# Moving four modulation chunks from TensorE to VectorE and sharing weight pieces between two streams at the ends of stages

## The chip, the cores and the metric

The kernel runs on one NeuronCore of a Trainium2 chip, as one program in one launch. The metric is the device time of that launch in microseconds (us). Of the core's engines TensorE (PE) multiplies matrices and transposes, VectorE (DVE) does elementwise work and row statistics, ScalarE (ACT) applies functions and scaled copies, GpSimd (POOL) does little here but issue some DMAs, and the sync engine (SP) issues the DMAs that bring weights from HBM.

## The reference

A first block (a hybrid attention layer, not touched here) makes x of 256 tokens x 1024 channels. Then a second block of two layers works on two streams, the latent x and a context of 256 tokens:

```python
for l in range(2):
    mod_l = silu(c) @ ada_w[l] + ada_b[l]        # 9 chunks of 1024: shift, scale, gate x 3; c is one vector
    mod_c = silu(c_ctx) @ ada_w[l] + ada_b[l]    # the same for the context
    xl = layer_norm(ALPHA*xl + 0.5*g1 * swiglu(xl*(1+sc1)+sh1, ffn1_w_in[l], ffn1_w_out[l]))
    xc = the same with the context's chunks
    yc, yl = even_mixer(...) if l == 0 else odd_mixer(...)     # linear attention + MLA, or neighbourhood attention
    xl = layer_norm(ALPHA*xl + g2 * yl)
    xl = layer_norm(ALPHA*xl + 0.5*g3 * swiglu(xl*(1+sc3)+sh3, ffn2_w_in[l], ffn2_w_out[l]))
    # in layer 0 xc takes the last two steps too; in layer 1 only xl does
```

All of it is in float32, with a hidden width of 2816 in the feed-forwards.

## The kernel before

**Streams and products.** X and C are the two streams, two tiles of 128 tokens each. In the code who=1 is C and who=0 is X; `order` is C first, then X. Every product is made of split numbers: a factor is a high part plus a low part, and `mm3` (L434 to L436) issues three matmuls for one product, high x high, low x high and high x low. A weight piece is 128 x 1024 floats, 512 KB. `wload` brings it: SP issues the DMA into `wr` (`wraw`), ACT casts it to `wh` (L353), DVE subtracts to get `wl` (L428), and then PE uses both. There are four buffers each of `wr`, `wh` and `wl`.

**Stages.** ff1 (name "f1", l=0), then the even mixer (`even_first`, scans, attention, and `mixer_out`), then ff2 (name "f2", l=0), then f1 of layer 1, the odd mixer (its value projection is `odd_values`), and f2 of layer 1 for X alone. `ffn_two` walks over 22 hidden tiles in groups of 8, 8 and 6. A call of `ffn_in` makes one hidden tile from two weight pieces; for both streams together (512 tokens) that is 48 matmuls of 128x512. In the first three hidden tiles of a stage (F0) the streams go one after the other at 256 tokens, and each loads the pieces for itself. `ffn_out` multiplies a group with the output weights, in two halves n=0 and n=1 of 512 channels.

**The end of a stage.** After the last group the kernel does C's n=0, C's n=1, then X's n=0, X's n=1, each with pieces of its own. `accum` (L571ff: L575 multiplies by the gate row, L579 or L577 adds to the stream), `layernorm` (L580ff: statistics L587, reciprocal root L367 to L377, normalisation L592) and `xt_mod` (L545ff: transposes L527 on PE, modulation L558, high part on ACT, low part XTL by L560) follow for each stream. For some streams (table `TL`) n=1 goes through `tail`, which takes the second tile in smaller column parts. `mixer_out` has the same shape with 8 pieces for each stream, `odd_values` with 8 for each stream too.

**Modulation.** A chunk (l, c) is 1024 columns of ada_w[l]. `ada` computes it on PE: 64 float32 matmuls with two useful rows (L620), and for a chunk that is no gate two transposes (L635). `ada_v` computes it on DVE: for each of 8 pieces two operations (L660, one for c and one for c_ctx) that multiply a 128x1024 piece by a broadcast row and sum along it; 16 in a chunk. Lists V1, V2 and V3 say which chunks DVE takes, in ff1, in ff2 of layer 0 and in f1 of layer 1. `fillv` takes VR[..][0] pieces after every `ffn_in` of the stage from the sixth on and VR[..][1] after steps of `ffn_out`; what is left of a list is emitted at the head of the stage's end (`self.fillv(1000)`). Chunks of neither list are taken by `fill`, on PE, in ff1 and in the even mixer.

**What sets the order.** The program is written in the order above, with `defer` moving `xt_mod` a few weight loads later. A scheduler of the tile framework then orders each engine's instructions by priority and estimated readiness; on the chip each engine works through its list in that order.

Of the kernel before, what the change touches and what calls it, by code (L numbers as in the profile page):

```python
# [20 lines left out]
P = 128  # L21
D = 1024
KD = 8
NFT = 22
# [178 lines left out]
GX = 0.0  # L203
DF = (3, 3, 3, 4, 2)
TL = (1, 0, 0, 0, 1, 1, 0, 0, 1)
# [13 lines left out]
ROWS = 1  # L219
# [24 lines left out]
class Kern:  # L244
# [95 lines left out]
    def need(self, l, c):  # L340

        while (l, c) not in self.done:
            if (l, c) in V1 + V2 + V3:
                self.fillv(1)
# [370 lines left out]
        for _ in self.ffn_in_steps(*a):  # L715
            pass

    def ffn_in_steps(self, wi, ft, hid, ts, hs, pool, tag, share=None):

        nc = self.nc  # L720
        N = ts.stop - ts.start
        if N == 256:
            b = self.bank(tag)
            pgu = (b[:, :256], b[:, 256:])
        else:
            pgu = (self.bank(tag), self.bank(tag))
        for j in range(2):
            h, lo = self.wload(wi, (2 * ft + j) * 1024, 1024, share)
# [8 lines left out]
        self.split(hid[:, 0, hs], hid[:, 1, hs], pgu[1])  # L737
        yield

    def ffn_out(self, wo, n, f0, f1, hid, tiles, tag, early={}):  # L740
# [25 lines left out]
        for (z, gb, c0), o in zip(tiles, outs):  # L766
            self.accum(z, n, o, gb, f0 == 0)

    def tail(self, rows, mul, gb, first, tag, done=None):


        nc = self.nc
        for m, z in enumerate(rows):
            st = self.small([P, 3, 6], "lnst3", bufs=2)
            nc.vector.bn_stats(st[:, 0], z[:, :512])
            parts = ((0, 256), (256, 512)) if m else ((0, 512),)
            for i, (a, b) in enumerate(parts):
                o = self.bank(tag)
                mul(o[:, a:b], m, a, b)
                t = o[:, a:b]  # L780
# [12 lines left out]
            nb = self.small([P, 1], "lnnb")  # L793
            nc.vector.scalar_tensor_tensor(nb, mv[:, 0:1], -1.0, y, op0=OP.mult, op1=OP.mult)
            h = slice(0, D)
            if m:
                h = slice(512, D)
                nc.vector.tensor_scalar(z[:, :512], z[:, :512], mv[:, 0:1], y, op0=OP.subtract, op1=OP.mult)
            self.act(z[:, h], z[:, h], AF.Identity, scale=y, bias=nb)
            if done:  # L800
                done(m)

    def ffn_tail(self, wo, f0, hid, tiles, done=None):

# [61 lines left out]
    def ffn_two(self, name, l, pool, order, after, fills=(0, 0), vr=(0, 0), early={}):  # L866


        self.pnext = PNF[2 * l + int(name[1]) - 1]
        gbs = {}  # L870
        wi, wo = self.A[name + "i"][l], self.A[name + "o"][l]
        G, F0 = 8, F2[l]
        if early:
            F0 = len(early) + FE
        for f0 in range(0, NFT, G):
            f1 = min(f0 + G, NFT)
            hid = []
# [3 lines left out]
            if f0 == 0:  # L881
                for w in order:
# [3 lines left out]
                    for ft in range(0 if w == 0 else len(early), F0):  # L886
                        self.ffn_in(wi, ft, hid[ft], ts, ts, pool, "B", GX)
# [30 lines left out]
    def mixer_out(self, src, l, who, pool):  # L918
        self.pnext = PN[4]
        gb = self.gate_rows(l, 1, who, pool)  # L920
        rows = (self.X, self.C)[who]
        outs = self.xs(src, 0, 512, 256 * who, 2)
        for m in range(2):
            self.accum(rows[m], 0, outs[m], gb, True)
        if TL[6 + who]:
            self.xs_tail(src, 4096, 256 * who, rows, gb)
        else:
            outs = self.xs(src, 4096, 512, 256 * who, 2, rows=ROWS)
            for m in range(2):
                self.accum(rows[m], 1, outs[m], gb, True)  # L930
            self.layernorm(rows)


    def rope(self, v, cos, sin, half, tag):
# [825 lines left out]

    def odd_values(self, e, order):
        V = [self.tl(e, [P, D], f"nv{m}") for m in range(4)]
        for w in order:
            for n in range(2):
                outs = self.xs(self.A["na"], 16 * 1024 + n * 4096, 512, 256 * w, 2)
                for m in range(2):
                    self.copy_any(V[2 * w + m][:, n * 512:(n + 1) * 512], outs[m])
        return V

    def odd(self, e, V):  # L1770
# [47 lines left out]
    def run(self):  # L1818
        tc, nc, A = self.tc, self.nc, self.A
        stage = self.stage or 99  # L1820
# [45 lines left out]
        with tc.tile_pool(name="xd", bufs=1) as xc:  # L1866
# [1 line left out]
            for i, t in enumerate(self.X + self.C):  # L1868
                nc.gpsimd.dma_start(t, save[i])
            with tc.tile_pool(name="mo", bufs=1) as g:  # L1870
                self.gbn, self.accp = 1, g
                self.mixer_out(A["evo"], 0, 1, g)
                if stage > 5:
                    self.defer(lambda: self.xt_mod(0, 6, 1), DF[2])
                self.mixer_out(A["evo"], 0, 0, g)
                if stage > 5:
                    self.defer(lambda: self.xt_mod(0, 6, 0), DF[3])
            if stage == 5:
                return self.store()
            self.gbn, self.phase = 2, 1  # L1880
# [10 lines left out]
            with tc.tile_pool(name="nm", bufs=1) as e:  # L1891
# [3 lines left out]
                with tc.tile_pool(name="na", bufs=1) as e2:  # L1895
                    V = self.odd_values(e2, (1, 0))
# [5 lines left out]
                gb = self.gate_rows(1, 1, 0, e)  # L1902
                outs = self.xs(A["nao"], 0, 512, 0, 2, xh=self.NH, xl=self.NL, tag="P")
# [4 lines left out]
                else:  # L1908
                    outs = self.xs(A["nao"], 4096, 512, 0, 2, xh=self.NH, xl=self.NL, tag="P", rows=ROWS)
# [78 lines left out]
```

## Time and profile before

| | us |
|---|---|
| median of 3 runs | 2183.82 (2181.91 to 2188.89) |
| the profiled execution, by its own clock | 2177.1 |
| its span from first to last instruction | 2175.3 |
| PE busy | 2097.1 (96%) |
| DVE busy | 1512.4 (70%) |
| ACT busy | 868.0 (40%) |

The profile is of one execution. Busy time is the time in which an engine's instructions run; PE is busy for nearly all of the span, so what PE is given to do, and the few places where it stands idle, make up the time. In the rows below, a number in square brackets behind an instruction is the time that its engine stood idle before it, with the event that ended the wait. [...]

### The profile page before, as it was taken

What the parts mean: (1) busy time and instruction counts of PE and PEld (TensorE: products, weight loads), DVE (VectorE), ACT (ScalarE), POOL (GpSimd) and SP (SyncE); (2) the same over time, 40 slices, a digit from 0 to 9 for tenths busy, and PEclk for the clock granted to TensorE, in tenths of its full rate; (3) what the DMA queues carried; (4) which work ended last, traced back from release to release, by engine and by line L of the source; (5) the groups of instructions that cost most, each with busy time, mean ns of one, the idle gap of its engine ahead of it and who ended that gap; (6) DMA issues with size and microseconds to landing.
All of it is one profiled execution on the core that took longest, in us unless ns stands there. A gap on an engine that the chain in (4) does not pass through costs nothing.

```text
span 2175.3 us, 31944 instructions
## 1 busy us (share of the span) xinstructions
PE 2097.1 (96%) x12484; PEld 1769.3 (81%) x12484; DVE 1512.4 (70%) x2746; ACT 868.0 (40%) x1493; POOL 40.0 (2%) x78
## 2 busy tenths in 40 slices
PE   7999999999999899998999999899999989998998
PEld 5898798888877787887888888888888868887997
DVE  6977866667778775868466656846665676776666
ACT  5555545222223534544322223532222255654443
POOL 1000000000000000000000000000000010000000
PEclk9999999999999999999999999999999999998999
DMA  8545547656665312347444545544453364424663
GB/s 283 194 149 177 158 145 245 205 176 202 201 203 178 100 57 67 119 147 240 134 126 146 164 118 154 174 126 136 140 170 113 110 188 145 105 86 138 188 182 123
DMA packets 94903, 337.84 MB, mean 155 GB/s; under 512 B 11357, under 2 KB 12477, under 8 KB 94753
## 3 DMA queue, kind: packets, MB, share of 16 engines
q1 hardware_dynamic: 87552, 314.78, 46.8%
q0 software_dynamic: 5856, 17.39, 2.7%
q10 hardware_dynamic: 1344, 3.64, 0.5%
q8 instruction: 98, 1.61, 0.3%
q14 instruction: 53, 0.43, 0.1%
HBM read 332.94 MB, written 3.20 MB: 155 GB/s over the span
## 4 chain that ended last, share of the span: by engine, by line
PE 87%; DVE 7%; DMA 2%; ACT 2%; issue 2%; SPq 0%; ACTq 0%; DVEq 0%
PE pB L434 13%; PE pB L436 12%; PE pB L435 12%; PE pA L436 10%; PE pA L435 10%; PE pA L434 10%; PE pB L1483 2%; PE pF L434 2%; PE pF L436 2%; PE pF L435 2%; DVE wl L428 1%; PE pP L434 1%; PE pP L435 1%; PE pP L436 1%; DMA wr<-in_ada_dram 1%
## 5 line engine op out<-in xcount | busy, mean ns | idle before, releaser
L353 ACT ACTIVATE wh<-wr 128x1024 fp32r<-128x1024 f32 (+4 forms) x460 | 480.2, 1047 | 1022.5 <-issue 490.8
L428 DVE TENSOR_TENSOR wl<-wr,wh 128x1024 fp32r<-128x1024 f32 (+4 forms) x460 | 553.1, 1204 | 335.6 <-ACT wh L353 332.2
L434 PE MATMUL pB<-XTH,wh 128*128 128x512 f32 (+1 forms) x1552 | 539.3, 348 | 6.8 <-DVE hid L441 4.0
L436 PE MATMUL pB<-XTH,wl 128*128 128x512 f32 (+1 forms) x1552 | 535.3, 345 | 5.6 <-DVE wl L428 5.6
L435 PE MATMUL pB<-XTL,wh 128*128 128x512 f32 (+1 forms) x1552 | 535.6, 345 | 0.4 <-DVE XTL L560 0.4
L434 PEld LDWEIGHTS pB<-XTH,wh 128*128 128x128 f32 x1552 | 294.5, 190 | 48.5 <-DVE hid L441 4.4
L436 PEld LDWEIGHTS pB<-XTH,wl 128*128 128x128 f32 x1552 | 294.5, 190 | 43.9 <-DVE wl L428 5.8
L435 PEld LDWEIGHTS pB<-XTL,wh 128*128 128x128 f32 x1552 | 294.4, 190 | 38.2 <-DVE XTL L560 0.6
L435 PE MATMUL pA<-wl,hid 128*128 128x512 f32 (+1 forms) x624 | 239.5, 384 | 2.6 <-DVE wl L428 2.6
L436 PE MATMUL pA<-wh,hid 128*128 128x512 f32 (+1 forms) x624 | 239.5, 384 | 0.0
L434 PE MATMUL pA<-wh,hid 128*128 128x512 f32 (+1 forms) x624 | 238.0, 383 | 0.0
L660 DVE SCALAR_TENSOR_TENSOR vj<-wr,cb 128x1024 f32<-128x1024 f32 x176 | 214.9, 1221 | 11.7 <-DMA wr<-in_adav_dram 8.3
L736 DVE TENSOR_TENSOR pB<-ft,pB 128x512 f32<-128x512 f32 (+1 forms) x97 | 55.7, 574 | 136.2 <-PE pB L436 134.9
L435 PEld LDWEIGHTS pA<-wl,hid 128*128 128x128 f32 x624 | 117.2, 188 | 27.3 <-DVE wl L428 3.8
L434 PEld LDWEIGHTS pA<-wh,hid 128*128 128x128 f32 x624 | 117.1, 188 | 24.9 <-issue 0.6
L436 PEld LDWEIGHTS pA<-wh,hid 128*128 128x128 f32 x624 | 117.2, 188 | 22.8
L435 PE MATMUL pA<-wl,XTH 128*128 128x512 f32 (+4 forms) x336 | 125.0, 373 | 5.6 <-DVE wl L428 5.5
L434 PE MATMUL pA<-wh,XTH 128*128 128x512 f32 (+4 forms) x336 | 125.6, 376 | 0.4 <-ACT wh L353 0.4
L436 PE MATMUL pA<-wh,XTL 128*128 128x512 f32 (+4 forms) x336 | 125.5, 374 | 0.0
L575 DVE TENSOR_TENSOR pA<-pA,gb 128x512 f32<-128x512 f32 x84 | 58.0, 695 | 31.9 <-PE pA L436 31.7
L435 PEld LDWEIGHTS pA<-wl,XTH 128*128 128x128 f32 x336 | 64.7, 193 | 17.3 <-DVE wl L428 6.9
L434 PEld LDWEIGHTS pA<-wh,XTH 128*128 128x128 f32 x336 | 64.9, 193 | 12.3 <-ACT wh L353 0.7
(456 smaller groups left out, 2949.3 us busy)
## 6 DMA issues: line engine op xcount, KB each, us to landing
wr<-in_f1i_dram SPq DMA_DIRECT2D x108, 512.0 KB, 4.4
wr<-in_f2i_dram SPq DMA_DIRECT2D x94, 512.0 KB, 4.0
wr<-in_adav_dram SPq DMA_DIRECT2D x88, 512.0 KB, 3.9
wr<-in_ada_dram SPq DMA_DIRECT2D x56, 512.0 KB, 4.3
wr<-in_f1o_dram SPq DMA_DIRECT2D x56, 512.0 KB, 3.7
wr<-in_f2o_dram SPq DMA_DIRECT2D x50, 512.0 KB, 3.6
wr<-in_w_dram SPq DMA_DIRECT2D x40, 512.0 KB, 4.3
wr<-in_na_dram SPq DMA_DIRECT2D x32, 512.0 KB, 3.6
```

The costliest lines, as they stand in the source:

```text
L353: self.lasta = self.nc.scalar.activation(out, in_, func, **kw)
L428: i = eng.tensor_sub(lo[:, :w], raw[:, :w], h[:, :w].bitcast(F32))
L434: nc.tensor.matmul(out, lh, rh, start=start, stop=False)
L435: nc.tensor.matmul(out, lh, rl, start=False, stop=False)
L436: self.lastmm = nc.tensor.matmul(out, ll, rh, start=False, stop=stop)
L575: nc.vector.tensor_mul(p, p, gb[:, cs])
L660: nc.vector.scalar_tensor_tensor(junk, raw, 0.5 * f, cb[:, w], op0=OP.mult, op1=OP.mult, accum_out=gc[:, w, k:k + 1])
L736: nc.vector.tensor_mul(pgu[1], t, pgu[1])
L1483: nc.tensor.matmul(p[:, c0 + j * P:c0 + (j + 1) * P], K[r, j * 256 + tk * P:j * 256 + (tk + 1) * P], Q[r, j * 256 + tq * P:j * 256 + (tq + ...
```

## The change

**Modulation.** Chunks (0,6), (0,7), (0,8) and (1,1), which PE computed, go to DVE: V1 has 6 chunks in place of 5, V2 has 4 in place of 3, V3 has 5 in place of 3. PE keeps only chunks (0,0) to (0,2), which are done during the first block. The rates rise from 2.0, 1.25 and 1.25 pieces to 2.4, 1.75 and 2.2.

**Weight pieces.** At the end of a stage the new `both_out` loads the pieces of n=0 once for C and X (`row_products`), and then the pieces of n=1 once, for C and then for X. So C's second half comes after X's first half. C's `xt_mod` is emitted at X's first product of n=1. `mixer_out` uses the same function and loads both gate rows ahead (`gbn` 2). In the first three hidden tiles of a stage the last tile's two pieces are kept from C for X (`keep`). `odd_values` makes C n=0, C n=1, X n=1 with C's pieces, and X n=0. In all 36 of 432 pieces of 128x1024 fall away.

```diff
-V1 = ((0, 3), (0, 4), (0, 5), (1, 0), (1, 2))
-V2 = ((1, 3), (1, 4), (1, 5))
-V3 = ((1, 6), (1, 7), (1, 8))
-VR = ((2.0, 0.5), (1.25, 0.25), (1.25, 0.25))
+V1 = ((0, 3), (0, 4), (0, 5), (0, 6), (0, 7), (0, 8))
+V2 = ((1, 0), (1, 1), (1, 2), (1, 3))
+V3 = ((1, 4), (1, 5), (1, 6), (1, 7), (1, 8))
+VR = ((2.4, 0.5), (1.75, 0.25), (2.2, 0.25))
...
+    def row_products(self, ws, mul, tiles, n, first, tag, hook=None):
+        for i, (z, gb, _) in enumerate(tiles):
+            o = self.bank(tag)
+            mul(o, i, 0, 512)
+            if hook and i == 0:
+                hook()
+            self.accum(z, n, o, gb, first)
+
+    def both_out(self, pieces, mul, streams, first, ends, tag, after):
+        ws = pieces(0)
+        alls = streams[0][1] + streams[1][1]
+        self.row_products(ws, lambda o, i, a, b: mul(ws, o, alls[i], a, b), alls, 0, first, tag)
+        w1 = pieces(1)
+        for i, (rows, tiles) in enumerate(streams):
+            def hook():
+                if i == 1:
+                    with self.tc.issue_after(self.lastmm.ins):
+                        after(0)
+            def m1(o, m, a, b):
+                mul(w1, o, tiles[m], a, b)
+            if ends[i]:
+                self.tail(rows, m1, tiles[0][1], first, tag, hook=hook)
+            else:
+                self.row_products(w1, m1, tiles, 1, first, tag, hook)
+                self.layernorm(rows)
+        after(1)
...
                 self.fillv(1000)
-                for w in order:
-                    for _ in self.ffn_out(wo, 0, f0, f1, hid, tiles(w), "A"):
-                        pass
-                    if TL[2 * (2 * l + int(name[1]) - 1) + w]:
-                        self.ffn_tail(wo, f0, hid, tiles(w))
-                    else:
-                        for _ in self.ffn_out(wo, 1, f0, f1, hid, tiles(w), "A"):
-                            pass
-                        self.layernorm((self.X, self.C)[w])
-                    self.defer(lambda w=w: after(w), DF[0] if w else DF[1])
+                us = range(f0, NFT, 2)
...
+                k = 2 * (2 * l + int(name[1]) - 1)
+                self.both_out(lambda n: [self.wload(wo, (n * NFT + u) * 512, 1024) for u in us], mul,
+                              [((self.X, self.C)[w], tiles(w)) for w in order], False, [TL[k + w] for w in order], "A",
+                              lambda i: self.defer(lambda: after(order[1]), DF[1]) if i else after(order[0]))
```

The instruction lists show the new order at three places. First DVE at the end of ff1, before. `vj` rows are operations of the modulation (here a gate chunk), `wl` rows the low parts of weight pieces, `lnst` the statistics of C's rows:

```order
L660 SCALAR_TENSOR_TENSOR vj_4862,vg_6570<-wr_6757,cb_4859 128x1024
L579 TENSOR_TENSOR C_4_98<-C_4_98,pA_6768 128x512
L660 SCALAR_TENSOR_TENSOR vj_4862,vg_6570<-wr_6757,cb_4859 128x1024
L428 TENSOR_TENSOR wl_6845<-wr_6841,wh_6843 128x1024
L666 SCALAR_TENSOR_TENSOR vg_6570<-adabc,vg_6570 128x16
L587 BN_STATS lnst_6888<-C_3_97 128x6
L587 BN_STATS lnst_6905<-C_4_98 128x6
L428 TENSOR_TENSOR wl_6927<-wr_6923,wh_6925 128x1024
```

The same place in the changed kernel, where the `pA` rows are the gate multiplications of C's second half:

```order
L660 SCALAR_TENSOR_TENSOR vj_4850,vg_6452<-wr_6545,cb_4847 128x1024
L428 TENSOR_TENSOR wl_6671<-wr_6667,wh_6669 128x1024
L660 SCALAR_TENSOR_TENSOR vj_4850,vg_6452<-wr_6545,cb_4847 128x1024
L428 TENSOR_TENSOR wl_6677<-wr_6673,wh_6675 128x1024
L660 SCALAR_TENSOR_TENSOR vj_4850,vg_6452<-wr_6549,cb_4847 128x1024
L587 BN_STATS lnst_6739<-C_4_98 128x6
L660 SCALAR_TENSOR_TENSOR vj_4850,vg_6452<-wr_6549,cb_4847 128x1024
L575 TENSOR_TENSOR pA_6679<-pA_6679,gb_4859 128x512
L666 SCALAR_TENSOR_TENSOR vg_6452<-adabc,vg_6452 128x16
L575 TENSOR_TENSOR pA_6700<-pA_6700,gb_4859 128x512
```

Eight operations of the modulation stood behind the last hidden tile of the stage (its L441) before, thirteen stand there now, and the kept pieces of n=1 (`wl_6671`, `wl_6677`) stand among the last of them. Second PE at the same place, before. `pF` with `ident` are transposes of C, `pA_7045` and `pA_7085` are X's second half:

```order
L434 MATMUL pA_7045<-wh_7033,hid_6243 128x512
L435 MATMUL pA_7045<-wl_7035,hid_6243 128x512
L527 MATMUL pF_6981<-ident,C_3_97 128x128
L527 MATMUL pF_6992<-ident,C_3_97 128x128
L436 MATMUL pA_7045<-wh_7033,hid_6243 128x512
L434 MATMUL pA_7045<-wh_7033,hid_6244 128x512
L435 MATMUL pA_7045<-wl_7035,hid_6244 128x512
L436 MATMUL pA_7045<-wh_7033,hid_6244 128x512
L434 MATMUL pA_7045<-wh_7039,hid_6245 128x512
L435 MATMUL pA_7085<-wl_7029,hid_6241 128x256
L436 MATMUL pA_7085<-wh_7027,hid_6241 128x256
```

And in the changed kernel, where `pA_6863` is the last part of X's second half and `pA_6909` and `pA_6940` belong to `even_first`:

```order
L435 MATMUL pA_6863<-wl_6677,hid_6065 128x256
L436 MATMUL pA_6863<-wh_6675,hid_6065 128x256
L527 MATMUL pF_6776<-ident,C_3_97 128x128
L527 MATMUL pF_6787<-ident,C_3_97 128x128
L527 MATMUL pF_6776<-ident,C_4_98 128x128
L527 MATMUL pF_6776<-ident,C_3_97 128x128
L527 MATMUL pF_6776<-ident,C_4_98 128x128
L527 MATMUL pF_6787<-ident,C_4_98 128x128
L527 MATMUL pF_6787<-ident,C_3_97 128x128
L527 MATMUL pF_6787<-ident,C_4_98 128x128
L434 MATMUL pA_6909<-XTH,wh_6905 32x256
L434 MATMUL pA_6940<-XTH,wh_6936 128x256
```

Before, C's transposes stood within X's products; now all of X's products stand ahead of them. Third DVE at the end of f1 of layer 1, before, where `pA_15367` is X's last column part and `wl_15425` the first piece of `odd_values`:

```order
L786 TENSOR_TENSOR X_1120_9407<-X_1120_9407,pA_15367 128x256
L560 TENSOR_TENSOR XTL<-pF_15274,XTH 128x256
L375 TENSOR_SCALAR nwt_15332<-nwy_15331,lnv_15329 128x1
L787 BN_STATS lnst_15343<-X_1120_9407 128x6
L376 TENSOR_SCALAR nwt_15332<-nwt_15332 128x1
L428 TENSOR_TENSOR wl_15425<-wr_15421,wh_15423 128x1024
L377 TENSOR_SCALAR nwy_15331<-nwt_15332,nwy_15331 128x1
L789 BN_AGGR lnmv_15389<-lnst_15343 128x2
L428 TENSOR_TENSOR wl_15443<-wr_15439,wh_15441 128x1024
```

And in the changed kernel, where `wl_14999` is the first piece of `odd_values` and `X_1064` X's second tile with its first half:

```order
L575 TENSOR_TENSOR pA_14670<-pA_14670,gb_12965 128x512
L579 TENSOR_TENSOR X_1063_9019<-X_1063_9019,pA_14670 128x512
L428 TENSOR_TENSOR wl_14722<-wr_14718,wh_14720 128x1024
L428 TENSOR_TENSOR wl_14728<-wr_14724,wh_14726 128x1024
L575 TENSOR_TENSOR pA_14691<-pA_14691,gb_12965 128x512
L428 TENSOR_TENSOR wl_14999<-wr_14995,wh_14997 128x1024
L579 TENSOR_TENSOR X_1064_9020<-X_1064_9020,pA_14691 128x512
L793 TENSOR_TENSOR pA_14732<-pA_14732,gb_12963 128x512
```

The first piece of `odd_values` stood behind X's last addition before; now it stands ahead of the end of X's first half, before anything of X's second half.

## Rows read from the trace of the kernel before

**Rows 1.** Page, part 1: busy us (share of the span) xinstructions.

```profile
PE 2097.1 (96%) x12484; PEld 1769.3 (81%) x12484; DVE 1512.4 (70%) x2746; ACT 868.0 (40%) x1493; POOL 40.0 (2%) x78
```

**Rows 2.** Four stretches of stages: length, busy us by engine, PEclk, DMA share, GB/s.

```profile
364.00:640.00 276.00, 276.00 (x1551) 228.38 (x1550) 193.37 (x278) 74.35 (x98) 0.50 (x1) 1.00 0.62 194
...
843.00:906.00 63.00, 60.78 (x495) 47.97 (x494) 48.56 (x91) 30.18 (x57) 1.14 (x2) 0.92 0.39 128
...
1026.00:1343.00 317.00, 316.57 (x1431) 259.98 (x1430) 191.41 (x260) 85.12 (x110) 0.50 (x1) 1.00 0.47 139
...
1404.00:1723.00 319.00, 319.00 (x1450) 261.35 (x1449) 192.09 (x260) 84.02 (x106) 0.50 (x1) 1.00 0.46 135
```

**Rows 3.** Line L620 alone in two stretches: PE and weight-load busy us (records).

```profile
340.00:668.00 328.00, 11.10 (x320) 8.26 (x320) 1.00 0.64 207
...
843.00:906.00 63.00, 8.76 (x192) 5.40 (x192) 0.92 0.39 128
```

**Rows 4.** PE in order of time around one burst of L620: start, duration, instruction.

```profile
642.21 0.39 PE L435 MATMUL pB<-XTL,wh 128*128 128x512 f32 x1
...
643.15 0.40 PE L436 MATMUL pB<-XTH,wl 128*128 128x512 f32 x1
643.47 1.08 PE L620 MATMUL pF<-wr,cs 128*32 128x128 f32 x32
...
644.82 0.39 PE L435 MATMUL pB<-XTL,wh 128*128 128x512 f32 x1
```

**Rows 5.** PE at the end of ff1, with its idle time in brackets.

```profile
684.13 0.49 PE L435 MATMUL pA<-wl,hid 128*128 128x512 f32 x1 [1.18 <-DVE wl L428]
...
711.72 0.55 PE L434 MATMUL pA<-XTH,wh 128*128 128x256 f32 x1 [3.56 <-DVE nwt L373]
```

**Rows 6.** DVE just ahead of that first wait.

```profile
681.71 1.22 DVE L660 SCALAR_TENSOR_TENSOR vj<-wr,cb 128x1024 f32<-128x1024 f32 x1
...
682.85 1.22 DVE L428 TENSOR_TENSOR wl<-wr,wh 128x1024 fp32r<-128x1024 f32 x1
```

**Rows 7.** DVE by line from 668 to 713.4 us: busy us, mean ns of one.

```profile
L428 DVE TENSOR_TENSOR wl<-wr,wh 128x1024 fp32r<-128x1024 f32 (+1 forms) x10 | 11.3, 1126 | 0.2 <-ACT wh L353 0.2
L660 DVE SCALAR_TENSOR_TENSOR vj<-wr,cb 128x1024 f32<-128x1024 f32 x8 | 9.8, 1219 | 0.0
L575 DVE TENSOR_TENSOR pA<-pA,gb 128x512 f32<-128x512 f32 x6 | 4.1, 692 | 0.0
L560 DVE TENSOR_TENSOR XTL<-pF,XTH 128x256 fp32r<-128x256 f32 x8 | 3.2, 417 | 0.1
...
L587 DVE BATCH_NORM_STATS2 lnst<-C 128x6 f32<-128x512 f32 x4 | 2.6, 680 | 0.0
...
L592 DVE TENSOR_SCALAR C<-C,lnmv,nwy 128x1024 f32<-128x1024 f32 x2 | 1.6, 804 | 0.0
...
L375 DVE TENSOR_SCALAR nwt<-nwy,lnv 128x1 f32<-128x1 f32 x3 | 0.8, 267 | 0.0
```

**Rows 8.** PE at the end of the even mixer, with its idle time.

```profile
1018.20 0.77 PE L527 MATMUL pF<-ident,X 128*128 128x128 f32 x5 [2.65 <-DVE X L592]
```

**Rows 9.** PE at the end of ff2 of layer 0, with its idle time.

```profile
1383.97 0.58 PE L436 MATMUL pB<-XTH,wl 128*128 128x256 f32 x1 [5.56 <-DVE wl L428]
```

**Rows 10.** PE at the end of f1 of layer 1 and in odd_values, with its idle time.

```profile
1763.74 0.80 PE L435 MATMUL pA<-wl,XTH 128*128 128x512 f32 x1 [5.00 <-DVE wl L428]
...
1782.12 0.88 PE L527 MATMUL pF<-ident,X 128*128 128x128 f32 x3 [3.98 <-DVE XTL L560]
```

**Rows 11.** ACT in that stretch: the cast of a piece of odd_values.

```profile
1773.08 1.06 ACT L353 ACTIVATE wh<-wr 128x1024 fp32r<-128x1024 f32 x1 [6.70 <-DMA wr<-in_na_dram]
```

**Rows 12.** Three stretches of 20 us around those ends, columns as in rows 2.

```profile
700.00:720.00 20.00, 14.90 (x99) 12.80 (x98) 18.27 (x50) 9.46 (x17) 1.75 (x5) 0.83 0.44 134
...
1380.00:1400.00 20.00, 16.02 (x116) 16.03 (x117) 18.29 (x43) 8.02 (x15) 0.00 (x0) 0.83 0.61 189
1760.00:1780.00 20.00, 14.41 (x56) 11.37 (x56) 12.98 (x33) 7.12 (x10) 5.26 (x9) 0.83 0.94 265
```

More of the change, by code (lines that the diff above doesn't have):

```diff
@@ L716, in ffn_in, with ffn_in_steps @@
             pass
-    def ffn_in_steps(self, wi, ft, hid, ts, hs, pool, tag, share=None):
+    def ffn_in_steps(self, wi, ft, hid, ts, hs, pool, tag, share=None, ws=None):
         nc = self.nc
         N = ts.stop - ts.start
+        new = []
         if N == 256:
@@ L727, in ffn_in_steps @@
         for j in range(2):
-            h, lo = self.wload(wi, (2 * ft + j) * 1024, 1024, share)
+            if ws and len(ws) == 2:
+                h, lo = ws[j]
+            else:
+                h, lo = self.wload(wi, (2 * ft + j) * 1024, 1024, share)
+                if ws is not None:
+                    new.append((h, lo))
             self.ws(pgu[j], h, lo, ts)
@@ L737, in ffn_in_steps @@
         self.split(hid[:, 0, hs], hid[:, 1, hs], pgu[1])
+        if new:
+            ws += new
         yield
@@ L767, in ffn_out, with tail @@
             self.accum(z, n, o, gb, f0 == 0)
-    def tail(self, rows, mul, gb, first, tag, done=None):
+    def tail(self, rows, mul, gb, first, tag, done=None, hook=None):
         nc = self.nc
@@ L779, in tail @@
                 mul(o[:, a:b], m, a, b)
+                if hook and m == 0:
+                    hook()
                 t = o[:, a:b]
@@ L881, in ffn_two @@
             if f0 == 0:
+                keep = []
                 for w in order:
@@ L885, in ffn_two @@
                         self.flush()
-                    for ft in range(0 if w == 0 else len(early), F0):
-                        self.ffn_in(wi, ft, hid[ft], ts, ts, pool, "B", GX)
+                    fs = list(range(0 if w == 0 else len(early), F0))
+                    if keep:
+                        fs = fs[-1:] + fs[:-1]
+                    for ft in fs:
+                        self.ffn_in(wi, ft, hid[ft], ts, ts, pool, "B", GX, keep if ft == F0 - 1 else None)
             for ft in range(f0 if f0 else F0, f1):
@@ L918, in mixer_out @@
-    def mixer_out(self, src, l, who, pool):
-        self.pnext = PN[4]
[L920 to L931, printed above, removed]
+                us = range(f0, NFT, 2)
@@ new lines, in mul @@
+                def mul(ws, o, t, a, b):
+                    for u, w in zip(us, ws):
+                        for j in range(2):
+                            hh, s = hid[u + j - f0], slice(t[2], t[2] + P)
+                            js = slice(j * 512 + a, j * 512 + b)
+                            self.mm3(o, hh[:, 0, s], hh[:, 1, s], w[0][:, js], w[1][:, js], u + j == f0, u + j == NFT - 1)
+                k = 2 * (2 * l + int(name[1]) - 1)
+                self.both_out(lambda n: [self.wload(wo, (n * NFT + u) * 512, 1024) for u in us], mul,
+                              [((self.X, self.C)[w], tiles(w)) for w in order], False, [TL[k + w] for w in order], "A",
+                              lambda i: self.defer(lambda: after(order[1]), DF[1]) if i else after(order[0]))
@@ new lines, in mixer_out, with mul @@
+    def mixer_out(self, src, l, pool, after):
+        self.pnext = PN[4]
+        streams = []
+        for w in (1, 0):
+            gb = self.gate_rows(l, 1, w, pool)
+            rows = (self.X, self.C)[w]
+            streams.append((rows, [(rows[m], gb, 256 * w + m * P) for m in range(2)]))
+        def mul(ws, o, t, a, b):
+            s = slice(t[2], t[2] + P)
+            for k in range(8):
+                w, js = ws[k // 2], slice(k % 2 * 512 + a, k % 2 * 512 + b)
+                self.mm3(o, self.XTH[:, k, s], self.XTL[:, k, s], w[0][:, js], w[1][:, js], k == 0, k == 7)
+        self.both_out(lambda n: [self.wload(src, n * 4096 + 1024 * u, 1024) for u in range(4)], mul, streams, True,
+                      (TL[7], TL[6]), "A", after)
@@ L1762, in odd_values, with put @@
         V = [self.tl(e, [P, D], f"nv{m}") for m in range(4)]
-        for w in order:
-            for n in range(2):
-                outs = self.xs(self.A["na"], 16 * 1024 + n * 4096, 512, 256 * w, 2)
-                for m in range(2):
-                    self.copy_any(V[2 * w + m][:, n * 512:(n + 1) * 512], outs[m])
+        src, o = self.A["na"], 16 * 1024
+        a, b = order
+        def put(w, n, outs):
+            for m in range(2):
+                self.copy_any(V[2 * w + m][:, n * 512:(n + 1) * 512], outs[m])
+        put(a, 0, self.xs(src, o, 512, 256 * a, 2))
+        ws = []
+        for w in (a, b):
+            outs = [self.pA(), self.pA()]
+            for u in range(4):
+                if w == a:
+                    ws.append(self.wload(src, o + 4096 + u * 1024, 1024))
+                elif u == 0:
+                    self.flush()
+                for m in range(2):
+                    s = slice(256 * w + m * P, 256 * w + (m + 1) * P)
+                    for j in range(2):
+                        js = slice(j * 512, (j + 1) * 512)
+                        self.mm3(outs[m], self.XTH[:, 2 * u + j, s], self.XTL[:, 2 * u + j, s], ws[u][0][:, js], ws[u][1][:, js],
+                                 u + j == 0, u == 3 and j == 1)
+            put(w, 1, outs)
+        put(b, 0, self.xs(src, o, 512, 256 * b, 2))
         return V
@@ L1870, in run @@
             with tc.tile_pool(name="mo", bufs=1) as g:
[L1871 to L1877, printed above, removed]
+                self.gbn, self.accp = 2, g
+                self.mixer_out(A["evo"], 0, g, lambda i: self.defer(lambda: self.xt_mod(0, 6, 0), DF[3]) if i
+                               else self.xt_mod(0, 6, 1))
             if stage == 5:
```

2 lines of the change are left out of this document (added).

## The prediction, as put on record

> **What bounds the kernel now.** I began with the page's busy times: PE is busy for 96% of the span, DVE for 70% [rows 1]. So time is won by giving PE less to do or by filling its gaps, and DVE has room on the average only. The next view was busy time by stretch. In the middle of the three feed-forwards that carry modulation on DVE, PE is busy for all of the time and DVE for 193.37 of 276, 191.41 of 317 and 192.09 of 319 us [rows 2]. Then PE in order of time with its idle gaps. These lie at the ends of stages, where one stream's last products, its layer norm, its transposes and the next stage's first product follow each other: 1.18 and 3.56 us at the end of ff1 [rows 5], 2.65 at the end of the even mixer [rows 8], 5.56 at the end of ff2 [rows 9], 5.00 and 3.98 around odd_values [rows 10]. All these end with something of DVE. Last, the clock there: it is granted at 0.83 on average over 20 us at three of the ends [rows 12], so PE fell to the lower of its levels for part of them, and (1 - 0.83) x 20 = 3.4 us of work is lost beside the gap, at most.
>
> **Modulation off PE.** A burst of L620 has 32 records. From the matmul before it (643.15) to the second one after it (644.82) pass 1.67 us [rows 4]; two 128x512 matmuls alone take 2 x 0.235 = 0.47, since four steps from 642.21 to 643.15 take 0.94 [rows 4]. So a burst costs 1.20 us, and a hidden tile of 48 matmuls takes 11.3 us. In ff1 320 records are 10 bursts, 12.0 us; in the stretch from 843 to 906 192 records are 6 bursts, 7.2 us [rows 3]. The six transposes of L635 that go too are priced from a row of L527, five of which take 0.77 us: 0.15 each, 0.9 in all [rows 8]. In ff1 PE is busy without a gap, so all of its 12.9 us count (between 12.0 and 13.5). In 843 to 906 PE works 60.78 of 63 us, at a clock of 0.92 [rows 2]: a chain of scans is near behind it. I take 5 of the 7.2, with 0 and 7.2 as ends.
>
> **Modulation onto DVE.** Four chunks are 64 operations of L660 at 1.22 us [rows 7], 78 us. They are hidden if DVE keeps ahead of PE. By stretch, one chunk more in ff1 and in ff2 is 16 x 1.22 = 19.5 us, two more in f1 of layer 1 are 39: DVE comes to 213 of 263, 211 of 317 and 231 of 319 us. Within ff1 it is tighter: at the rate 2.4 a hidden tile brings 4.8 operations of L660 (5.9 us), two subtractions of L428 (2.4) and three 128x512 operations at about the 0.69 us of L575 (2.1) [rows 7], 10.4 us beside 11.3 of PE, 92%. The cover is the four buffers of each weight part, about two pieces or one hidden tile ahead. I charge 3 us, three waits of the size that the end of ff1 shows (1.18) [rows 5], with 0 below and the rival's price above.
>
> Here a row speaks against the change. The subtraction for which PE waited at 684.13 ran from 682.85 and stood behind a modulation operation that began at 681.71 [rows 5, 6]. [...]
>
> **Fewer weight pieces.** 36 subtractions (36 x 1.22 = 44 us of DVE), as many casts at 1.06 us [rows 11] (38 us of ACT) and 18 MB of DMA go. PE's matmuls stay, so all of this counts only where a piece was late. With the 78 us DVE's sum grows by 34. What the reuse moves is the order at four ends; one half of one stream is 36 matmuls there, 36 x 0.235 = 8.5 us (mixer 48, 11.3 us). Before, C's second half was followed by both of X's, 16.9 us (22.6), beside which C was normalised and transposed; now by X's second half alone, 8.5 (11.3). What C needs after its last product: two multiplications and two additions (4 x 0.69), two statistics (2 x 0.68), two normalisations (2 x 0.80) [rows 7] and a chain of nine short operations, at no more than the 0.27 us of L375 each [rows 7] 2.4 us: 8.1 us, without anything between.
>
> End of ff1: 8.1 of need against 8.5 of cover is even, but five more modulation operations lie ahead (5 x 1.22 = 6.1 us), while six subtractions fewer (7.3 us) are spread over the whole end. All of C's transposes now stand behind X's products, with the eight XTL (8 x 0.42 = 3.3) behind them [rows 7], where half of them lay among X's products. Between 0 (DVE's sum is the same) and +8.5 (all the cover lost) I take +4. The old gap of 3.56 stays.
> Even mixer: the cover of 11.3 still exceeds 8.1 and no modulation runs there; but X's own wait of 2.65 stays [rows 8] and C's last XTL join it. I take +2, less than one such wait more, between 0 and two of them (+5).
> End of ff2, layer 0: the gap of 5.56 ends with a subtraction [rows 9] that stood behind X's statistics; fewer pieces let the first of them come earlier, while C now stands later. -1.5 between -9.0 (5.56 and 3.4 of clock) and +3.
> End of f1, layer 1: 5.00 + 3.98 + 3.4 = 12.4 us are lost [rows 10, 12]. Before, the first piece of odd_values was subtracted behind X's last addition, and ACT waited 6.70 us for a later piece to land [rows 11]. Six pieces fewer ahead let the DMAs start earlier, and the subtraction now stands before X's second half. I take the 5.00 and 2 of the 3.4 as won, -7, between -12.4 and 0; what is late next is C's XTL, as at 1782.12.
>
> **The sum**, against the profiled execution of 2177.1 us: -12.9 - 5 + 3 + 4 + 2 - 1.5 - 7 = -17.4, so 2159.7. The median of the runs shown is 2183.8, 6.7 above that execution; so the forecast is 2166.
>
> **Rivals.** First, slower: VectorE's queue. The place is the three feed-forward stages, 276 + 317 + 319 = 912 us or 81 lengths of 11.3 us. If subtractions come late behind modulation operations, each length gets a wait. For: the 92% above and rows 5 and 6. Against: PE never waited in those stretches at DVE loads of 60 to 70% [rows 2]. From 0.25 us per length on (20.4 us without the 3 charged, over 81) it eats the whole gain; at 0.4 us it costs 32, which is +12 on the sum: 2195.
> Second, no change: the scan stretch gives 0 of its 5, C's lost cover costs its upper ends (+8.5 and +5), ff2's end +3 and odd_values nothing, since its pieces still land late [rows 11]: -12.9 + 0 + 3 + 8.5 + 5 + 3 + 0 = +6.6 with all of these at their ends; with the three ends half way to them from what I take, +6.2, +3.5 and +0.8, and nothing else won, it is +0.6 less 2 for part of odd_values: -1.4, 2182. For: every one of these gaps ends with DVE, which gets busier. Against: PE's 12.9 us in ff1 are work on the critical path, and nothing takes its place.
> Third, more: the gaps at the ends of ff2 and f1 close with the clock staying up, -9.0 and -12.4, the scan stretch gives 7.2, and ff1's end costs nothing: -12.9 - 7.2 + 2 - 9.0 - 12.4 = -39.5, less some for a new wait: 2148. For: each of these two ends waits for one subtraction that is queued late. Against: C's chain is the next to be late at each.
> [...]
>
> **Chances.** The forecast's case 0.60 (its own range 2152 to 2177), the third 0.14, the second 0.14, the first 0.12. What can be told from no change is about 0.3%, 6.5 us. Faster: the third, nearly all of the forecast's case (0.57) and a little of the second, 0.73. Same: most of the second and the rest of the forecast's, 0.16. Slower: the first, less its mildest part, 0.11. For 8 in 10 the range goes from 2147, where the third case lies, to 2188, beyond the second; part of the first is left out.
>
> **What would show it.** L620 keeps 384 records, all before 340 us. If the forecast holds, the middle of ff1 is some 12 us shorter with PE still busy throughout, and the waits of PE on L428 in all three feed-forwards add up to less than 5 us; many small gaps behind L428 there would be the first rival. At the end of ff1 PE's gap before even_first grows from 3.56 to about 8 us. At odd_values the gap of 5.00 behind L428 is gone, and a wait on C's XTL stays. The stretch from 843 to 906 falls by some 5 us; if not at all, the second case. I am wrong if DVE's load beside PE's lets subtractions slip, or if C's chain, now with half its cover, becomes the longest wait at all four ends.

## The result, and the profile after

The changed kernel takes 2154.22 us (median of 4 runs, 2154.07 to 2158.79) against 2182.86 for the kernel before (4 runs, 2180.84 to 2188.89): ratio 0.9869, 95% interval 0.9846 to 0.9893, 28.6 us less. Forecast were 2166 and a range of 2147 to 2188. Its profiled execution took 2154.17 us, its median; the one of before lay 5.8 us below its median, so the two spans differ by 22.9 us only.

The page of the changed kernel, part 1, with the columns of [rows 1]:

```profile
PE 2080.7 (97%) x11967; PEld 1759.8 (82%) x11967; DVE 1548.6 (72%) x2834; ACT 829.4 (39%) x1450; POOL 36.8 (2%) x73
```

PE's busy time fell by 16.4 us, DVE's rose by 36.2 (the estimate was 34) and ACT's fell by 38.6. Where the time went is best seen between matmuls that both kernels have. The table gives the length of each stretch in us, from the start times of such matmuls on PE. "ff1 middle" runs from the first feed-forward matmul to the first of ff1's last output group; "ff1's end" from there to the first matmul of the attention; "scans" on to the first of the even mixer's output; "mixer" on to the second output group of ff2; "ff2 middle" on to ff2's last output group; "ff2's end" to the first output group of f1 in layer 1; "f1 middle" to its last; "odd" to the first matmul of layer 1's attention; "rest" to the end of the last matmul.

| stretch | before | changed | difference | forecast |
|---|---|---|---|---|
| first block | 338.5 | 341.7 | +3.2 | 0 |
| ff1 middle | 329.5 | 316.9 | -12.6 | -12.9 |
| ff1's end | 96.5 | 97.7 | +1.1 | +4 |
| scans | 191.2 | 183.9 | -7.3 | -5 |
| mixer | 276.2 | 277.1 | +0.9 | +2 |
| ff2 middle, f1 middle | 356.0 | 355.9 | -0.1 | up to +3, with ff1's |
| ff2's end | 135.2 | 131.0 | -4.2 | -1.5 |
| odd | 95.5 | 91.7 | -3.8 | -7 |
| rest | 348.3 | 348.4 | +0.1 | 0 |

Without the first block the changed kernel is 25.9 us shorter in the trace. The first block has the same work in both; in the ten profiles of this study it took between 338.5 (before) and 345.2 us, so I do not count its +3.2 as part of the change, and without it the trace comes near the 28.6 us of the medians.

The middle of ff1, as in the first of [rows 2]: PE still has no gap, and DVE is busy for 207.10 us in place of 193.37 over the same 276. The number behind POOL's is PEclk, TensorE's granted clock as a share of full speed; in the kernel before it reads 1.00 from 704 to 706 us and 0.50 from 712 to 716.

```profile
364.00:640.00 276.00, 276.00 (x1348) 230.72 (x1347) 207.10 (x298) 76.69 (x98) 0.50 (x1) 1.00 0.58 175
```

PE's gaps at the ends, in order of time (they answer to [rows 5], [rows 8] and [rows 10]; the number in brackets is the idle time ahead of the row):

```profile
694.72 0.48 PE L527 MATMUL pF<-ident,C 128*128 128x128 f32 x1 [2.73 <-DVE C L592]
...
705.19 0.42 PE L436 MATMUL pA<-XTH,wl 128*32 128x256 f32 x1 [2.48 <-DVE wl L428]
...
1000.66 0.39 PE L434 MATMUL pB<-XTH,wh 128*128 128x256 f32 x1 [3.79 <-DVE hid L441]
...
1756.39 0.48 PE L527 MATMUL pF<-ident,X 128*128 128x128 f32 x1 [5.58 <-ACT X L353]
```

At the end of ff1 PE waits for C's normalisation, as was forecast, and then for a low part; the sum is about that of before. The gap of 5.56 at the end of ff2 [rows 9] has shrunk, the longest there being 0.87, and the 5.00 behind L428 in front of odd_values [rows 10] is gone. In its place stands a wait of 5.58 for X's normalisation. ACT, in order of time, shows what made that late:

```profile
1754.15 1.06 ACT L353 ACTIVATE wh<-wr 128x1024 fp32r<-128x1024 f32 x1 [9.65 <-DMA wr<-in_na_dram]
1755.11 1.22 ACT L353 ACTIVATE X<-X,lnnb,nwy 128x1024 f32<-128x1024 f32 x1
```

The normalisation stood on ACT behind the cast of a piece of odd_values that had not landed; its own last input (`lnnb`, L805 on DVE) was done at 1748.0. The DMA of that piece, and what POOL issued just ahead of it:

```profile
1740.75 4.96 POOL L1866 DMA_DIRECT2D nb<-in_bias_dram  x8 [29.13 <-DVE XTL L560]
...
1744.75 0.33 SPq L394 DMA_DIRECT2D wr<-in_na_dram  x1
```

The piece was there at the cast, 9.4 us after its issue, where the median of the 28 transfers from `in_na_dram` is 3.7. The eight loads of the odd mixer's bias ahead of it are 256 KB each, and before the change they stood in the same place. That they made the piece late is argued from this order; no run moved them.

### The profile page after: what moved, and what is told of

Read it like the earlier page. It is cut to its first block, busy times and chain, and to the rows that moved or that the text cites. A ratio compares the mean times of both kernels' runs of the same rounds, so it can differ in the third digit from the quotient of the medians.

```text
span 2152.4 us, 30804 instructions
## 1 busy us (share of the span) xinstructions
PE 2080.7 (97%) x11967; PEld 1759.8 (82%) x11967; DVE 1548.6 (72%) x2834; ACT 829.4 (39%) x1450; POOL 36.8 (2%) x73
## 4 chain that ended last, share of the span: by engine, by line
PE 87%; DVE 6%; ACT 2%; issue 2%; DMA 2%; SPq 0%; ACTq 0%; DVEq 0%
PE pB L434 13%; PE pB L435 13%; PE pB L436 13%; PE pA L434 10%; PE pA L435 10%; PE pA L436 10%; PE pF L434 2%; PE pF L436 2%; PE pF L435 2%; PE pB L1536 1%; PE pP L434 1%; PE pP L435 1%; PE pP L436 1%; DVE wl L428 1%; ACT wh L353 1%
## 5 line engine op out<-in xcount | busy, mean ns | idle before, releaser
L353 ACT ACTIVATE wh<-wr 128x1024 fp32r<-128x1024 f32 (+4 forms) x424 | 442.1, 1045 | 1011.7 <-issue 460.0
L428 DVE TENSOR_TENSOR wl<-wr,wh 128x1024 fp32r<-128x1024 f32 (+4 forms) x424 | 509.4, 1203 | 303.6 <-ACT wh L353 300.3
L434 PE MATMUL pB<-XTH,wh 128*128 128x512 f32 (+1 forms) x1552 | 538.2, 348 | 10.5 <-DVE hid L441 6.4
L660 DVE SCALAR_TENSOR_TENSOR vj<-wr,cb 128x1024 f32<-128x1024 f32 x240 | 293.0, 1221 | 4.0
L434 PEld LDWEIGHTS pA<-wh,hid 128*128 128x128 f32 x624 | 117.2, 188 | 22.9
```

The lines of the kernel that those rows point to most:

```text
L353: self.lasta = self.nc.scalar.activation(out, in_, func, **kw)
L428: i = eng.tensor_sub(lo[:, :w], raw[:, :w], h[:, :w].bitcast(F32))
L434: nc.tensor.matmul(out, lh, rh, start=start, stop=False)
L660: nc.vector.scalar_tensor_tensor(junk, raw, 0.5 * f, cb[:, w], op0=OP.mult, op1=OP.mult, accum_out=gc[:, w, k:k + 1])
```

## The experiments

**The lists alone, and the shared pieces alone.** The first question was whether TensorE's saved work makes the gain.

```diff
 # e1_lists_only: the kernel before
-V1 = ((0, 3), (0, 4), (0, 5), (1, 0), (1, 2))
+V1 = ((0, 3), (0, 4), (0, 5), (0, 6), (0, 7), (0, 8))     (V2, V3 and VR as in the change)
 # e2_pieces_only: the changed kernel
+V1 = ((0, 3), (0, 4), (0, 5), (1, 0), (1, 2))             (V2, V3 and VR as before)
```

> The kernel before with the new lists and rates alone: the four chunks go from TensorE to VectorE, no weight piece is shared. Theory A (TensorE's work on the path is all that counts, and VectorE has room for 78 us more): the trace of the changed kernel against before shows the middle of ff1 11.6 us shorter and the scan stretch 7.3 us shorter; both come here too, and the ends stay as before or lose up to 4 us at the end of ff1 with its five more modulation operations: ratio to before 0.991 to 0.993 (-19 to -15 us). Theory B (the shared pieces make the room on VectorE for the modulation): without them subtractions come late, PE waits on L428 in the feed-forwards by more than 10 us in all, ratio 0.996 or more.

> The changed kernel with the old lists and rates: the pieces are shared and the order at the ends is the new one, but TensorE computes the four chunks again. Theory A: the two halves add up, so this keeps what the trace shows at the ends (ff2's end -3.7, f1 and odd_values -3.9, mixer +0.5): -7 us, ratio 0.997, with the 512 records of L620 back and ff1's middle as long as before. Theory B: sharing alone frees VectorE and ScalarE at the ends and is worth more without the modulation: -12 us or more, ratio 0.9945 or less.

Measured: the lists alone 0.9969 (0.9957 to 0.9981), some 7 us; the pieces alone 0.9895 (0.9871 to 0.9919), some 23 us. So theory A, which had -19 to -15 and -7, falls in its sizes; but the two do add up (7 and 23 against 28.6 for both). Theory B had both numbers. The pieces alone are worth over three times the lists alone. By stretch, as differences from before:

| stretch | lists alone | pieces alone | both |
|---|---|---|---|
| ff1 middle | -12.5 | -0.4 | -12.6 |
| ff1's end | +9.8 | -8.2 | +1.1 |
| scans | -7.2 | -5.6 | -7.3 |
| mixer | +1.6 | +1.5 | +0.9 |
| ff2's end | -0.6 | -4.4 | -4.2 |
| odd | +2.1 | -3.0 | -3.8 |

TensorE's saved work is there in full in the middle of ff1. But the end of ff1 gives 9.8 us of it back. Theory B had the place wrong: in the feed-forwards' middles nothing is late. At that end the lists alone put fourteen operations of L660 (17.0 us) into 32 us of a DVE that is busy for 31.41 of them:

```profile
L660 DVE SCALAR_TENSOR_TENSOR vj<-wr,cb 128x1024 f32<-128x1024 f32 x14 | 17.0, 1216 | 0.1
L428 DVE TENSOR_TENSOR wl<-wr,wh 128x1024 fp32r<-128x1024 f32 x6 | 7.2, 1207 | 0.2 <-ACT wh L353 0.2
```

These are DVE's lines from 662 to 694 us. PE, in the same kernel, stops again and again, here for a subtraction, for a cast and for an addition to C (L579):

```profile
679.16 0.50 PE L435 MATMUL pA<-wl,hid 128*128 128x512 f32 x1 [1.78 <-DVE wl L428]
...
684.48 0.47 PE L434 MATMUL pA<-wh,hid 128*128 128x512 f32 x1 [1.18 <-ACT wh L353]
...
687.87 0.58 PE L434 MATMUL pA<-wh,hid 128*128 128x256 f32 x1 [2.93 <-DVE C L579]
```

What this costs is seen over the whole end of ff1 (before, lists alone, pieces alone; length, then busy PE, weight loads, DVE, ACT, POOL, then PEclk):

```profile
668.01:764.55 96.54, 86.07 (x459) 68.91 (x456) 82.64 (x167) 43.78 (x62) 5.04 (x10) 0.96 0.40 125
...
662.10:768.45 106.35, 89.82 (x457) 71.23 (x455) 90.11 (x179) 44.91 (x62) 3.30 (x7) 0.92 0.39 124
...
673.04:761.34 88.30, 84.04 (x459) 67.74 (x456) 77.28 (x161) 37.32 (x56) 5.03 (x10) 1.00 0.33 104
```

PE stands idle for 10.5, 16.5 and 4.3 us. So of the +9.8 of the lists alone 6.1 are idle time, and 3.7 are the same matmuls at a lower granted clock (0.92 in place of 0.96). With the pieces alone, PE has little idle time there, and the clock stays up, as two stretches of 20 us show:

```profile
680.00:700.00 20.00, 20.00 (x89) 16.34 (x88) 19.44 (x40) 2.70 (x4) 0.51 (x1) 1.00 0.26 80
700.00:720.00 20.00, 18.50 (x138) 16.33 (x138) 18.51 (x57) 9.36 (x17) 2.66 (x6) 1.00 0.43 140
```

Before, the second of these had 14.90 of 20 us and a clock of 0.83 [rows 12]. The order in which C's second half comes behind X's first half is in this kernel too, and no wait of PE for C's normalisation comes with it.

The -5.6 of the scans, where L620 is back with its 192 records, is the clock's. Over that whole stretch (before, pieces alone, changed kernel):

```profile
764.55:955.76 191.21, 187.68 (x1321) 157.71 (x1321) 133.69 (x284) 91.86 (x210) 3.85 (x7) 0.95 0.27 85
...
761.34:946.99 185.65, 181.62 (x1320) 153.09 (x1320) 132.08 (x283) 90.56 (x209) 4.36 (x8) 0.98 0.28 87
...
756.21:940.11 183.90, 177.02 (x1125) 151.49 (x1125) 131.55 (x280) 89.60 (x206) 3.13 (x6) 0.95 0.18 53
```

With the pieces alone as many matmuls as before keep PE busy for 6.1 us less, at a granted clock of 0.98 in place of 0.95. In the stretch from 860 to 880 us this kernel (first row) was granted 1.00 and the changed kernel (second) 0.74, as before the change:

```profile
860.00:880.00 20.00, 18.30 (x148) 14.98 (x152) 19.14 (x34) 9.27 (x17) 1.14 (x2) 1.00 0.53 172
```

```profile
860.00:880.00 20.00, 17.24 (x96) 15.16 (x98) 16.69 (x29) 8.58 (x14) 0.00 (x0) 0.74 0.26 80
```

(1.00 - 0.74) x 20 is 5.2 us. Between the kernel before and the changed one the clock of the whole stretch is alike. There PE's busy time falls by 10.7 us, of which 8.8 are L620's own [rows 3], and its idle time rises from 3.5 to 6.9, which makes the -7.3.

**Own pieces for each stream, in the new order.** This tells the pieces from the order.

```diff
-        ws = pieces(0)
-        alls = streams[0][1] + streams[1][1]
-        self.row_products(ws, lambda o, i, a, b: mul(ws, o, alls[i], a, b), alls, 0, first, tag)
-        w1 = pieces(1)
+        for i in range(2):
+            ws, ts = pieces(0), streams[i][1]
+            self.row_products(ws, lambda o, m, a, b: mul(ws, o, ts[m], a, b), ts, 0, first, tag)
         for i, (rows, tiles) in enumerate(streams):
+            w1 = pieces(1)
```

> The changed kernel, but each stream loads pieces of its own again at the ends of feed-forwards and of the even mixer, in the new order (C first half, X first half, C second half, X second half); 26 of the 36 pieces come back, the first hidden tiles and odd_values keep their sharing. Theory A (a piece less counts only where the subtraction for it was the one that ended last): the ends of ff1, ff2 and f1 of layer 1 each get 6 subtractions of 1.22 us back on a VectorE that is busy there, +3 to +6 us each, ratio to before about 0.993. Rival C (the order alone makes the difference, the subtractions lie beside other work): within 3 us of the changed kernel, ratio 0.986 to 0.988.

Measured: 0.9924 (0.9901 to 0.9948), 12 us above the changed kernel by the ratios. Against the changed kernel the end of ff1 is 9.3 us longer and the end of ff2 5.3; the mixer is 1.5 shorter, odd 1.3 longer. So the saved pieces are the gain at these ends, and six of them, whose subtractions take 7.3 us, were worth more than that at the end of ff1; theory A, with 3 to 6 us at each of three ends, had too little there and too much at the third. A piece is a DMA, a cast and a subtraction; that the subtraction counts is argued from DVE's load, no run tells the three apart. Rival C falls. This run also prices the order by itself: it has the lists and, at the ends, the pieces of the run of the lists alone, and its end of ff1 stands at +10.5 against +9.8 there.

**The gate chunk later.** If the operations left over are what costs, they can be taken away from that end.

```diff
 # e6_gate_later: the changed kernel
-V1 = (..., (0, 6), (0, 7), (0, 8));  V2 = ((1, 0), ...);  VR = ((2.4, 0.5), (1.75, 0.25), ...)
+V1 = (..., (0, 6), (0, 7));  V2 = ((0, 8), (1, 0), ...);  VR = ((2.4, 0.5), (2.2, 0.25), ...)
 # e7_gate_sooner: and with it
-                if f0 or ft >= VS:
+                if f0 or ft >= (3 if name == "f2" else VS):
```

> The changed kernel with gate chunk (0,8) moved from the list of ff1 to the head of the list of ff2, whose rate goes from 1.75 to 2.2 pieces: no modulation is left for the end of ff1, where fourteen operations ran in the changed kernel. Theory A: C is normalised up to 6 us earlier there, and PE's gaps of 2.73, 0.81 and 2.48 us at that end fall by some 4 us in all; VectorE in ff2 rises by 19.5 us of 317 and nothing waits: 4 us less than the changed kernel, ratio to before 0.985. Rival D (the gate row is late in ff2, or VectorE's queue is): PE gets a new wait of several us at the first output group of ff2, ratio 0.988 or more.

Measured: 0.9871 (0.9847 to 0.9895), no gain over the changed kernel; the ratio lies between theory A's and rival D's, and the new wait of rival D is there. The end of ff1 is 7.6 us shorter than in the changed kernel, and the mixer's stretch 6.6 us longer, with one gap of PE in ff2:

```profile
1101.47 0.77 PE L434 MATMUL pA<-wh,hid 128*128 128x512 f32 x1 [8.08 <-DVE C L577]
```

L577 is the addition that needs the gate row of that very chunk. The next run starts the chunk two hidden tiles sooner.

> As the run with gate chunk (0,8) in the list of ff2, but the modulation of ff2 starts at the fourth hidden tile in place of the sixth. That run won 7.6 us at the end of ff1 and lost them in one gap of PE of 8.08 us before the first output group of ff2, where the gate row was late. If that gap is the chunk's lateness, two hidden tiles (22.6 us) sooner remove it, and the time falls by some 7 us, ratio to before 0.9835. If the gap has another cause (the DMA of the gate row behind others, the banks that the output holds), it stays and the ratio is 0.987.

Measured: 0.9830 (0.9802 to 0.9858), median 2144.21. The gap is gone, the mixer's stretch is back (+0.3 against before) and the end of ff1 is 8.0 us shorter than before. The lateness of the chunk was the cause. Its profiled execution has the scans 4.0 us shorter than the changed kernel's too. That is the clock: it was 0.98 there in place of 0.95, and PE was busy for 172.91 us in place of 177.02, with the same idle time.

**A higher rate in ff1.** The other way to leave less over.

```diff
-VR = ((2.4, 0.5), ...)
+VR = ((2.7, 0.5), ...)      e8: the changed kernel; e9: the kernel before with the new lists
```

> The changed kernel with the rate of ff1 at 2.7 pieces a hidden tile in place of 2.4, so that six operations of the modulation are left behind the last hidden tile in place of thirteen; VectorE's load beside PE rises to 11.1 of 11.3 us. Theory E (what the earlier runs point to: the leftover operations at the end of ff1 cost what the modulation gains in the middle; lists alone lost 9.8 us there, both halves 1.1, sharing alone won 8.2): the stretch from the end of ff1 to the attention falls by 4 to 7 us against the changed kernel, and the middle of ff1 stays within 1 us, ratio to before 0.984. Rival (VectorE has no room in the middle of ff1): the middle of ff1 grows by 2 us or more and eats it, ratio 0.987 or more.

> The kernel before with the new lists and the rate 2.7, no sharing of weight pieces. Theory E: the +9.8 us that the lists alone lost at the end of ff1 were the leftover operations; with six in place of thirteen it is +2 or less, the rest as in the run of the lists alone, ratio to before 0.993. Rival (without the shared pieces VectorE is late at that end whatever is left over): the end of ff1 still loses 6 us or more, ratio 0.996.

Measured: 0.9831 (0.9810 to 0.9851), median 2144.14, and 0.9917 (0.9897 to 0.9936). In the first the middle of ff1 kept its length (316.6 us against 316.9) at the higher load, and its end fell by 7.5 us against the changed kernel. The load itself is below the 11.1 of 11.3 us that I had reckoned: in 84 us of ff1's second group (first the changed kernel, then this one) DVE is busy for 83% and 88%, PE for all of the time.

```profile
461.00:545.00 84.00, 84.00 (x362) 67.57 (x361) 69.44 (x102) 23.42 (x30) 0.00 (x0) 1.00 0.63 191
...
461.00:545.00 84.00, 84.00 (x361) 67.43 (x360) 74.16 (x113) 23.45 (x30) 0.00 (x0) 1.00 0.66 202
```

DVE's lines from 654.8 to 690 us in this kernel:

```profile
L660 DVE SCALAR_TENSOR_TENSOR vj<-wr,cb 128x1024 f32<-128x1024 f32 x7 | 8.5, 1216 | 0.0
L428 DVE TENSOR_TENSOR wl<-wr,wh 128x1024 fp32r<-128x1024 f32 (+1 forms) x5 | 5.3, 1060 | 0.6 <-ACT wh L353 0.6
```

In the second the lists alone lose nothing at that end (-1.0 in place of +9.8), and their worth rises from 7 to some 18 us, near what TensorE's saved work comes to. Theory E holds in both. In e8 PE no longer waits for C's normalisation at that end, where the changed kernel waits 2.73 and 0.81 us. Each of the two versions, e7 and e8, is some 8 us faster than the changed kernel by the ratios (0.9830 and 0.9831 against 0.9869), though their intervals still overlap with its own.

**One operation more for each hidden tile.** What does VectorE's time cost beside a busy PE?

```diff
                     self.fillv(vr[0])
+                    self.extra(vr[0])     # one scalar_tensor_tensor of 128x1024, its result unused
```

> The changed kernel with one more VectorE operation of 128x1024 elements, of L660's kind and result unused, after each hidden tile that takes modulation pieces. Theory L (VectorE costs time only where its work beside a hidden tile exceeds PE's 11.3 us): ff1 comes to 10.4 + 1.2 = 11.6 us and loses 0.3 for each of 15 hidden tiles, some 5 us; ff2 (10.0) and f1 of layer 1 (11.1) lose nothing, +5 in all, ratio to before 0.989. Rival Q (the queue in order: every operation ahead of a needed subtraction is paid whatever the load): 0.5 us or more for each of some 45 hidden tiles, +20 us or more, ratio 0.996.

Measured: 0.9884 (0.9860 to 0.9907). The 49 operations take 59.7 us of DVE:

```profile
L682 DVE SCALAR_TENSOR_TENSOR vx<-cb 128x1024 f32<-128x1024 f32 x49 | 59.7, 1219 | 2.7 <-DMA cb<-srow 2.3
```

But the operation reads `cb` alone, so nothing ties it to its hidden tile, and by the trace they did not run beside one tile each: 15 start between 355.6 and 395.0 us, at the head of ff1, and 34 between 1009.1 and 1097.3, at the head of ff2; none runs in f1 of layer 1. So the run does not test the two theories' prices by the tile, and that the middles of ff2 and f1 did not change says nothing of them. By the ratios the time is 3 us above the changed kernel's, within the intervals; by the stretches 7.8.

What it does show is DVE at its fullest beside PE. In the 46 us with 19 of these operations PE has no gap:

```profile
1040.00:1086.00 46.00, 46.00 (x200) 37.30 (x199) 44.62 (x50) 12.66 (x16) 0.00 (x0) 1.00 0.39 114
```

Rival Q, by which each of them would be paid whatever the load, falls there. At the head of ff1 one of them was paid: it started on DVE at 360.00, ahead of the split of a hidden tile (L441 at 361.47), and PE waited for that:

```profile
362.02 0.55 PE L434 MATMUL pB<-XTH,wh 128*128 128x256 f32 x1 [2.36 <-DVE hid L441]
```

That gap is the 2.2 us by which the middle of ff1 is longer.

## Why the prediction was right, point by point

**The direction and the range held, for partly other reasons than given.** The forecast was -17.4 against the profiled execution; the stretches give -25.9.

**Modulation off PE: right.** -12.6 for -12.9 in ff1. In the scans -7.3 for -5: the bursts were worth more there than the 7.2 I had priced them at (PE's busy time fell by 10.7), and 3.3 us of that turned into idle time of PE, so work behind PE did take a part, as I had said.

**Modulation onto DVE: mis-sized.** The 3 us charged for late subtractions in the middles were nothing, and the first rival with them: in the three middles PE waits for no low part, at the load that I put at 92% and that measures 83% in ff1, at 88% (e8), and in 46 us of ff2 at 97% (e4). The row that I set against the change (1.18 us behind a modulation operation) [rows 5, 6] lies at the end of ff1. DVE ran there in the order of its list, in the kernel before (L660 at 681.71 us, L428 at 682.85, L666 at 683.99, L587 at 684.07) and in the changed one (L660 at 678.33, L428 at 679.47, L660 at 680.61, L428 at 681.75). At that end operations ahead of others cost: the five more that I counted are 6.1 us, I took 4 for the whole end, and the lists alone lost 9.8. In the middles, where low parts are made ahead into four buffers, they cost nothing; that the buffers are the reason is argued, since no run changed their number.

**End of ff1: right in the sum, the terms mis-sized.** +1.1 for +4. "DVE's sum is the same" was nearly what came: by the trace fourteen operations of the modulation start behind the stage's last hidden tile in place of eight, six more where I counted five, against six subtractions fewer. But I took the two sides as small: the runs show +9.8 for the operations and about -9 for the pieces. That the two meet near nothing, within the range I gave, is in part luck. C's halved cover costs nothing by itself: with the pieces alone C has the same 8.5 us of cover and PE does not wait for its normalisation, and the new order with own pieces adds 0.7 to the lists alone. It counts with the operations ahead of C, as I had it: with fourteen PE waits 3.5 us for C, with six (e8) not at all. The gap before even_first did not grow from 3.56 to 8; its longest is 2.48, behind the 2.73 for C. DVE was the bound of this stretch before the change. The stretch of [rows 7], read as a window, says so (length, then PE, weight loads and DVE busy):

```profile
668.00:713.40 45.40, 37.73 (x189) 30.55 (x185) 44.56 (x97) 17.09 (x27) 3.97 (x8) 0.96 0.46 148
```

With DVE busy for 44.56 of 45.40 us, more for DVE counts nearly in full there: six operations more, 7.3 us, made 6.1 us more of idle time on PE, and the lower clock another 3.7.

**Mixer: right in the size alone.** +0.9 for +2. X's own wait of 2.65, which I let stay, is down to 0.2, and a new one of 3.79 for a hidden tile of ff2 (L441) stands behind it; own pieces are 1.5 us better there in the one trace.

**End of ff2: mis-sized.** -4.2 for -1.5. I let C's later half eat most of the gap; PE does not wait for C's normalisation there, and 1.9 us of waits are left in all. The pieces did it (-4.4 with them alone, +1.1 without them in the new order, where PE does wait 3.7 us for C).

**odd_values: half right.** The 5.00 went, as forecast. The step that failed is that six pieces fewer let the DMAs start early enough: I named C's XTL as next to be late, but it was X's normalisation, 5.58 us, queued on ACT behind a piece that landed late, and so -3.8 came for -7. My second rival had late pieces here, and my sum had no term for the bias loads that are issued ahead of that piece.

**The median.** I carried the offset of 6.7 us between the profile of before and its median over to the changed kernel. The changed kernel's profile stands at its median; the profile of before had the shortest first block of all ten. That makes 3 us or so of the difference between 2166 and 2154.

## What to carry to other kernels

Divide the kernel into stretches and ask of each which engine bounds it, before pricing a change: the same modulation operation cost nothing beside PE-bound feed-forwards (ff1's middle took 316.6 us at the rate 2.7 and 316.9 at 2.4) and more than its own duration, with the lower clock, at an end that VectorE bounded (9.8 us for six more of them, 7.3 us of VectorE). Two halves of a change that each look like a gain may meet in one stretch and nearly cancel there, so test them apart. A probe operation that depends on nothing goes where the scheduler likes (here all 49 at the heads of two stages): look in the trace where it ran. Work that was spread by a rate was cheap here as long as its remainder did not fall into the handover between stages; a slightly higher rate was worth some 8 us by the ratios.

## What was not expected of the hardware

The first block, whose program is alike, took from 338.5 to 345.2 us in ten profiles, a spread as large as several of the terms; single profiles are to be compared by stretches. And the granted clock in the stretch from 860 to 880 us was 0.74 in two kernels and 1.00 in a third with PE busy for nearly as long there (18.25 us in 20 before, 18.30 in the third), which moved that stretch by 5 us. The same instants hold somewhat different work in the three, since each reaches this stretch at its own time. What set the clock there stays open.
